# A decoder trunk on one core: second key group in two portions, attention's stores later, one split moved to VectorE

## The chip, the cores and the metric

The kernel runs on one core of one Trainium2 chip. A core has five engines, each with its own queue of instructions: TensorE (PE in the profile; PEld is its weight load), VectorE (DVE), ScalarE (ACT), GpSimd (POOL) and SyncE (SP), which here issues nearly all DMAs. The metric is the device time of one execution in microseconds (us); a kernel's time is the median of its runs.

## The reference, cut to what matters

The reference is one layer of a hybrid decoder over 2048 tokens of width 1024. All is fp32.

```python
u = x * (1.0 + scale[:, None, :]) + shift[:, None, :]
h = u @ w_in[l]
q, k, v, a_gate, p_in, p_gate, m_a, m_p = jnp.split(h, offsets, axis=-1)
a = sliding_window_sink_attention(q, k, v, sinks[l], bias, mask) * jax.nn.silu(a_gate)
a = a @ w_attn_proj[l]
p = jnp.einsum('bsgc,gcd->bsgd', multiscale_causal_pool(p_in), w_pool_mix[l]).reshape(B, S, POOL_WIDTH)
p = (p * pool_scale[l]) * jax.nn.silu(p_gate)
p = p @ w_pool_proj[l]
y = jax.nn.sigmoid(m_a) * a + jax.nn.sigmoid(m_p) * p
y = (y @ w_out[l]) * (1.0 + gate[:, None, :])
x = layer_norm(DEEPNORM_ALPHA * x + y, ln_gain[l], ln_bias[l])
```

Attention has 16 query heads of width 64 and 2 groups of keys and values, each shared by 8 query heads. A block of 128 queries sees its own block of 128 keys and the one before, with a bias by distance and a sink term in the softmax.

## The kernel before, in words

Every large matrix product is done by a seven-product scheme for 2 x 2 blocks (Winograd's form of Strassen's), and each fp32 operand is cut into a high and a low part, so that a product of two blocks is three TensorE passes (hi x hi, hi x lo, lo x hi, in `mm3`). The activations for one contraction stand in seven "sets" (`B11`, `T1`, `T2`, `B21`, `T3`, `B22`, `T4`), each with high and low parts. The weights of two output columns of 128 form a `Quad`. A quad passes through four stages: F (products with B11 and T1), S (T2, B21), Th (T3, B22) and L (T4). Each product is 12 matmuls of 128 x 512.

Before a stage's products, `split_part` cuts that stage's raw weights (tile `W`, or `A` for the last stage) into a high part by ScalarE and a low part `w_set<-W,w_set` by another engine: VectorE, but GpSimd for stage Th of quads that run alone. The sums that a stage needs (`W<-W`, `W<-W,A`) are GpSimd's. `plan` fixes, ahead of time, at which product each split, load and sum is given out. Every engine keeps to the order in which the program gives instructions out.

The sequence of 2048 tokens is done as two chunks of 1024 (s = 0 and 1). For each chunk there is a start phase, a middle phase `o` in which 13 quads run alone while attention is laid between their matmuls (`overlay`), and an end phase with quads in pairs; phases for the output projections and the norm follow. In `overlay` a `beat` comes after every three matmuls of a product, and some of the beats run one `step(n)` of attention. There are 64 steps for pairs of heads and blocks of 128 queries (plus three to run out): scores of n, transposes of n-2, values of n-3. The tile names are `lg` for scores, `L` for softmax rows, `pt` for transposes, `pv` for values, `st` for finished outputs, `kk` and `vv` for keys and values, `qs` for queries and `bt` for the bias.

The keys of one group lie in one buffer `kk` (one copy). Steps 0 to 31 use group 0 and steps 32 to 63 group 1. After step 31 `load_k(1)` gives out the loads of group 1 into the same buffer, and eight beats pass before step 32 is given out; the loads themselves wait until the scores of step 31 have read the old keys. After step 34 the same is done for `vv`. A tile's 64 + 64 partitions hold high and low parts for scores in two passes; in chunk 1 a tail of 128 columns of chunk 0's keys stands ahead of the chunk's 1024.

When four blocks of a pair of heads are done, `finish` multiplies by the gate (GpSimd, `st<-st,ag`), makes the sums that the later projection's sets need (`st<-st`), and gives out the stores `ain_d<-st` with `defer(ticks, ...)`: a tick is one product. SyncE takes its queue in order, so a store whose data are not ready holds back what stands behind it.

Of the kernel before, what the change touches and what calls it, by code (L numbers as in the profile page):

```python
# [19 lines left out]
P = 128  # L20
D = 1024
# [6 lines left out]
HD = 64  # L28
# [31 lines left out]
def kernel(  # L60
# [89 lines left out]
    def low(engine, dst, src, hi):  # L150
        engine.tensor_tensor(dst, src, as32(hi), ALU.subtract)
# [186 lines left out]
    def plan(phases):  # L338

        products, before, stages, order = [], {}, [], []  # L340
        for phase in phases:
            phase["base"], last = None, None
            for gi, grp in enumerate(phase["groups"]):
                if gi == 0:
                    phase["first"] = len(products)
                for x, q in enumerate(grp):
                    q.x, q.pair, q.own = x, len(grp) > 1, len(grp) > 1 and gi % 2 == 1
                    order.append(q)
                for kind, names in STAGES:
                    if kind == "S" and gi == 0:  # L350
                        phase["base"] = len(products)
                    if kind == "S" and gi == len(phase["groups"]) - 1:
                        phase["turn"] = len(products)
                    for q in grp:
                        if kind == "L" and not q.pair:
                            last = q
                            continue
                        p = len(products)
                        q.at[kind] = p
                        for h, name in enumerate(names):  # L360
                            products.append((q, kind, h, name))
                            if last and kind == "F" and h == 0:
                                last.at["L"] = len(products)
                                products.append((last, "L", 0, "T4"))
                        stages.append((q, kind, p, len(products) - 1))
                        if last and kind == "F":
                            stages.append((last, "L", last.at["L"], last.at["L"]))
                            last = None
            if last:
                last.at["L"] = len(products)  # L370
                stages.append((last, "L", len(products), len(products)))
                products.append((last, "L", 0, "T4"))
            phase["end"] = len(products)
# [43 lines left out]
    def split_part(ph, q, kind, part):  # L417
        raw = {"F": q.first, "S": q.second, "Th": q.third, "L": lambda: q.a22}[kind]()
        if kind == "L":
            if part == 0:  # L420
                t = q.parts["L"] = ph.split(*q.rings[kind])
                act.copy(t[:, 0:CH], raw)
            else:
                t = q.parts["L"]
                low(dve, t[:, CH:], raw, t[:, 0:CH])
            return
        if part == 0:
            hi, lo = q.parts[kind] = [ph.split(x) for x in q.rings[kind]]
            act.copy(by_two(hi), raw)
            return  # L430
        hi, lo = q.parts[kind]
        low(pool if kind == "Th" and not q.pair else dve, by_two(lo), raw, by_two(hi))
        if kind == "F":
            q.mid(pool)
            defer(2, lambda q=q: q.keep_sum(1))
        if kind == "S":
            q.late(pool)
# [299 lines left out]
    def overlay(ph, s, n_slots):  # L737
# [7 lines left out]
        def load_k(kv):  # L745
            k = kvt["k"] = tp.tile([P, 2, D + s * P], F32R, tag="kk", bufs=1, name="kk")
            mine = slice(kv * HD, (kv + 1) * HD)
            for half in range(2):
                at = slice(half * HD, (half + 1) * HD)
                if s:  # L750
                    sp.dma_start(as32(k[at, :, 0:P]), k_d[0, mine, :, D - P :])
                sp.dma_start(as32(k[at, :, s * P :]), k_d[s, mine])

        def load_v(kv):
            v = kvt["v"] = tp.tile([P, 2 * NB + s, P], F32R, tag="vv", bufs=1, name="vv")
# [63 lines left out]
        def finish(j, t):  # L819
            x, gate = outs[j, t], ags.pop((j, t))  # L820
            i, half = j // 2, j % 2
            pool.tensor_tensor(x, x, gate, ALU.mult)
            if (half, t) == (0, 1):
                b11 = outs[j, 0]
                pool.tensor_tensor(x, x, b11, ALU.subtract)
            if (half, t) != (1, 1):
                name = {(0, 0): "B11", (0, 1): "T1", (1, 0): "B21"}[half, t]
                defer(1, lambda: ain_d[s].put(name, i, x), True)
                return
            b11, t1, b21 = (outs.pop(z) for z in ((j - 1, 0), (j - 1, 1), (j, 0)))  # L830
            outs.pop((j, 1))
            pool.tensor_tensor(t1, x, t1, ALU.subtract)
            pool.tensor_tensor(b11, t1, b11, ALU.subtract)
            pool.tensor_tensor(b21, b21, t1, ALU.subtract)
            for name, z in (("B22", x), ("T2", t1), ("T3", b11), ("T4", b21)):
                defer(1, lambda name=name, z=z: ain_d[s].put(name, i, z), True)

        def step(n):
            lg = scores(n) if n < N else None
# [672 lines left out]
```

## Time and profile before

| | us |
|---|---|
| median of 3 runs | 1764.14 (1763.76 to 1764.63) |
| profiled execution, its own time | 1761.28 |
| its span, first to last instruction | 1759.5 |
| TensorE busy in it | 1673.6 |
| VectorE busy | 1276.9 |
| ScalarE busy | 939.8 |
| GpSimd busy | 591.2 |

Times inside the profile count from the first instruction. Attention of chunk 0 runs from about 176 to 517 us, of chunk 1 from about 776 to 1106 us. Nearly all operations pass through one helper, so they all carry line L56 and are told apart by their tiles. The mean granted TensorE clock of the profiled execution was 0.985 of full speed.

### The profile page before, as it was taken

The page shows a single profiled execution, that of the slowest core. Times are in us where ns is not written, and L with a number is a line of the kernel's source. Part 1 is how long each engine was busy: PE and PEld are TensorE (multiplying, and loading weights), DVE is VectorE, ACT ScalarE, POOL GpSimd, SP SyncE. Part 2 cuts the span into 40 slices and gives each one's busy share as a digit, 9 for nine tenths or more (in the row PEclk, how much of TensorE's full clock was granted, in tenths as well). Part 3 has the DMA queues.
Part 4 walks back from the last instruction along what each step waited for, and adds up shares of the span by engine and source line. Part 5 has one row for each costly group of instructions (what it writes and reads, how often), then busy time and mean ns, then how long its engine had stood idle before and what let it go on. Part 6 is the DMA issues. An engine that isn't in the chain of part 4 may idle for free.

```text
span 1759.5 us, 24784 instructions
## 1 busy us (share of the span) xinstructions
PE 1673.6 (95%) x8061; PEld 1399.2 (80%) x8061; DVE 1276.9 (73%) x2325; ACT 939.8 (53%) x1796; POOL 591.2 (34%) x564
## 2 busy tenths in 40 slices
PE   6899899999989999999999999999999999999996
PEld 5687688788878888888887888788888888888774
DVE  5854687677865879658786888387876785877677
ACT  3643587667763345447766676334544353435441
POOL 3022344454553322423333343322243211124442
PEclk9899899999999999999999999999999999999998
DMA  9288768666646889783555544489968686785332
GB/s 347 96 278 284 186 200 253 212 209 205 214 152 203 274 260 334 251 274 131 167 177 178 174 145 155 152 275 321 340 236 299 218 311 218 245 285 199 144 144 108
DMA packets 237010, 389.50 MB, mean 221 GB/s; under 512 B 21824, under 2 KB 90704, under 8 KB 236624
## 3 DMA queue, kind: packets, MB, share of 16 engines
q1 hardware_dynamic: 235664, 386.29, 65.9%
q10 hardware_dynamic: 1184, 1.60, 0.3%
q8 instruction: 63, 1.03, 0.2%
q14 instruction: 67, 0.55, 0.1%
q0 software_dynamic: 32, 0.02, 0.0%
HBM read 243.63 MB, written 147.35 MB: 222 GB/s over the span
## 4 chain that ended last, share of the span: by engine, by line
PE 63%; DVE 13%; DMA 7%; issue 6%; ACT 6%; POOL 2%; SPq 1%; POOLq 0%; DVEq 0%; ACTq 0%
PE mm L56 39%; PE lg L56 11%; PE c L56 8%; DVE w_set L56 3%; PE pt L56 3%; PE pv L56 3%; DVE L L56 2%; DVE wide L56 2%; ACT L L56 2%; ACT w_set L56 1%; SPq L56 1%; DMA q_d<-q_hi 1%; DMA wide<-in_xr_dram 1%; DVE set_T L56 1%; DVE p L56 1%
## 5 line engine op out<-in xcount | busy, mean ns | idle before, releaser
L56 PE MATMUL mm<-set_B,w_set 128*128 128x512 f32 x2664 | 654.9, 392 | 0.7 <-DVE w_set L56 0.6
L56 PEld LDWEIGHTS mm<-set_B,w_set 128*128 128x128 f32 x2664 | 498.7, 189 | 104.0 <-DVE w_set L56 1.0
L56 POOL TENSOR_TENSOR W<-W 128x512 f32<-128x512 f32 x185 | 267.7, 1457 | 590.7 <-DVE w_set L56 380.6
L56 PE MATMUL mm<-set_T,w_set 128*128 128x512 f32 x1824 | 454.8, 396 | 5.1 <-POOL w_set L56 4.4
L56 PEld LDWEIGHTS mm<-set_T,w_set 128*128 128x128 f32 x1824 | 341.8, 191 | 76.9 <-POOL w_set L56 5.3
L56 DVE TENSOR_TENSOR w_set<-W,w_set 128x1024 fp32r<-128x1024 f32 x196 | 253.5, 1293 | 113.9 <-ACT w_set L56 105.9
L56 ACT CAST w_set<-W 128x1024 fp32r<-128x1024 f32 x222 | 232.2, 1047 | 79.5 <-PE mm L56 52.6
L56 ACT ACTIVATE L<-L 128x257 f32<-128x257 f32 (+3 forms) x384 | 191.2, 500 | 120.1 <-DVE L L56 119.4
L56 PE MATMUL lg<-set_T,w_set 128*128 128x512 f32 x864 | 212.0, 393 | 6.4 <-ACT w_set L56 4.0
L56 PE MATMUL c<-set_T,w_set 128*128 128x512 f32 x864 | 211.1, 393 | 5.0 <-ACT w_set L56 2.9
L56 PEld LDWEIGHTS lg<-set_T,w_set 128*128 128x128 f32 x864 | 162.8, 190 | 43.4 <-ACT w_set L56 4.8
L56 PEld LDWEIGHTS c<-set_T,w_set 128*128 128x128 f32 x864 | 162.1, 189 | 41.6 <-ACT w_set L56 4.5
L56 POOL TENSOR_TENSOR W<-W,A 128x512 f32<-128x512 f32 x41 | 55.5, 1353 | 281.4 <-DMA A<-in_win_dram 115.5
L56 DVE CUSTOM_DVE_ANT_0 L<-lg,bt,nsink 128x256 f32<-128x256 f32 (+1 forms) x256 | 111.0, 469 | 26.6 <-PE lg L56 19.8
L56 PEld LDWEIGHTS lg<-kk,qs 128*128 128x128 f32 x512 | 76.7, 190 | 49.1 <-DVE L L56 26.1
L56 PE MATMUL lg<-kk,qs 128*128 128x256 f32 (+1 forms) x512 | 84.2, 287 | 30.0 <-DVE L L56 17.1
L56 DVE TENSOR_TENSOR ptl<-pt,pth 128x512 fp32r<-128x512 f32 (+1 forms) x128 | 85.8, 670 | 30.9 <-ACT pth L56 30.2
L56 DVE TENSOR_SCALAR L<-L 128x256 f32<-128x256 f32 (+1 forms) x128 | 98.2, 767 | 4.5
L56 ACT ACTIVATE sig<-mm 128x512 f32<-128x512 f32 x76 | 45.5, 599 | 92.7 <-PE mm L56 88.1
L56 ACT CAST pth<-pt 128x512 fp32r<-128x512 f32 (+1 forms) x128 | 72.3, 565 | 27.9 <-PE pv L56 27.1
L56 POOL TENSOR_TENSOR w_set<-W,w_set 128x1024 fp32r<-128x1024 f32 x26 | 63.3, 2435 | 56.5 <-ACT w_set L56 36.8
L56 PE MATMUL pt<-ident,L 128*128 128x128 f32 x496 | 77.9, 279 | 0.0
(203 smaller groups left out, 1943.9 us busy)
## 6 DMA issues: line engine op xcount, KB each, us to landing
W<-in_win_dram SPq DMA_DIRECT2D x40, 512.0 KB, 5.9
qs<-q_d SPq DMA_DIRECT2D x128, 128.0 KB, 4.3
sums_d<-W SPq DMA_DIRECT2D x62, 256.0 KB, 4.3
W<-sums_d SPq DMA_DIRECT2D x31, 512.0 KB, 3.7
ain_d<-st SPq DMA_DIRECT2D x56, 256.0 KB, 2.5
A<-in_win_dram SPq DMA_DIRECT2D x42, 256.0 KB, 5.4
ag_d<-sig SPq DMA_DIRECT2D x32, 256.0 KB, 4.6
q_d<-q_hi SPq DMA_DIRECT2D x32, 256.0 KB, 3.9
```

The lines of the kernel that those rows point to most:

```text
L56: return lambda *args, **kw: self.tc.keep_in_program_order(op(*args, **kw))
```

## The change

It has three parts.

1. `load_k`: for group 1 the keys are loaded in two portions. The first has columns 0 to 255 of the chunk (two blocks) for both halves of the partitions, the second the other 768. For group 0 nothing is cut. In chunk 1 the two tails of 128 columns now stand ahead of the rest.
2. `finish`: the stores of the sets B11, T1 and B21 come 2 ticks after `finish` rather than 1. Of the last four, B22 stays at 1, T3 and T2 come at 2 and T4 at 3, with T3 ahead of T2.
3. `plan` marks the quads of a phase's last group as `tail`; `split_part` gives the low part of stage Th of such a quad to VectorE, where it ran alone and so was GpSimd's. That is one quad in each chunk's attention phase. Quads in pairs had VectorE already.

```diff
+                    q.tail = gi == len(phase["groups"]) - 1
...
-        low(pool if kind == "Th" and not q.pair else dve, by_two(lo), raw, by_two(hi))
+        low(pool if kind == "Th" and not q.pair and not q.tail else dve, by_two(lo), raw, by_two(hi))
...
-            for half in range(2):
-                at = slice(half * HD, (half + 1) * HD)
-                if s:
+            ats = [slice(half * HD, (half + 1) * HD) for half in range(2)]
+            if s:
+                for at in ats:
                     sp.dma_start(as32(k[at, :, 0:P]), k_d[0, mine, :, D - P :])
-                sp.dma_start(as32(k[at, :, s * P :]), k_d[s, mine])
+            cut = 2 * P if kv else 0
+            for a, b in ((0, cut), (cut, D)):
+                for at in ats if a < b else ():
+                    sp.dma_start(as32(k[at, :, s * P + a : s * P + b]), k_d[s, mine, :, a:b])
...
-                defer(1, lambda: ain_d[s].put(name, i, x), True)
+                defer(2, lambda: ain_d[s].put(name, i, x), True)
...
-            for name, z in (("B22", x), ("T2", t1), ("T3", b11), ("T4", b21)):
-                defer(1, lambda name=name, z=z: ain_d[s].put(name, i, z), True)
+            for name, z, ticks in (("B22", x, 1), ("T3", b11, 2), ("T2", t1, 2), ("T4", b21, 3)):
+                defer(ticks, lambda name=name, z=z: ain_d[s].put(name, i, z), True)
```

SyncE's queue at the change of keys in chunk 0 (`kk` keys, `sums_d` kept weight sums, `ag_d` the attention gate; - is before, + now):

```order
 L56 DMA bt<-e_rep 128x2x256
-L56 DMA kk<-k_d 64x2048 x2
-L56 DMA sums_d<-W 128x512
-L56 DMA ain_d<-st 128x512
-L56 DMA ag_d<-sig 128x512 x2
+L56 DMA kk<-k_d 64x2x256 x2
+L56 DMA kk<-k_d 64x2x768 x2
+L56 DMA sums_d<-W 128x512
+L56 DMA ag_d<-sig 128x512
+L56 DMA ain_d<-st 128x512
+L56 DMA ag_d<-sig 128x512
 L56 DMA sums_d<-W 128x512
```

Two DMAs have become four, and a store of attention stands one place later.

VectorE at the end of chunk 0's attention, where the last quad's splits stand (`o` is the part of `pv` that ScalarE copied, `p` a partial sum). Before:

```order
L56 TENSOR_TENSOR w_set<-W,w_set 128x1024
L56 TENSOR_TENSOR ptl<-pt,pth 128x512
L56 TENSOR_TENSOR st<-pv,o_5278 64x128 x2
L56 TENSOR_TENSOR st<-pv,o_5306 64x128 x2
L56 TENSOR_TENSOR mm<-mm,p_5319 128x512
L56 TENSOR_TENSOR w_set<-A_4854,w_set 128x512
L56 TENSOR_TENSOR w_set<-W,w_set 128x1024
```

And now:

```order
L56 TENSOR_TENSOR w_set<-W,w_set 128x1024
L56 TENSOR_TENSOR ptl<-pt,pth 128x512
L56 TENSOR_TENSOR st<-pv,o_5280 64x128 x2
L56 TENSOR_TENSOR st<-pv,o_5308 64x128 x2
L56 TENSOR_TENSOR w_set<-W,w_set 128x1024
L56 TENSOR_TENSOR mm<-mm,p_5321 128x512
L56 TENSOR_TENSOR w_set<-A_4856,w_set 128x512
L56 TENSOR_TENSOR w_set<-W,w_set 128x1024
```

The added split stands between attention's last outputs and the accumulation `mm<-mm,p`; GpSimd's queue has lost the same instruction behind its three `st<-st`.

SyncE's queue at the same place, before:

```order
L56 DMA ma_d<-sig 128x512
L56 DMA ain_d<-st 128x512 x4
L56 DMA W<-in_win_dram 128x512
L56 DMA W<-in_win_dram 128x2x512
L56 DMA u_d<-ux 128x4x256
L56 DMA A_5374<-in_win_dram 128x512
```

And now:

```order
L56 DMA ma_d<-sig 128x512
L56 DMA ain_d<-st 128x512
L56 DMA W<-in_win_dram 128x512
L56 DMA W<-in_win_dram 128x2x512
L56 DMA u_d<-ux 128x4x256
L56 DMA ain_d<-st 128x512 x2
L56 DMA A_5375<-in_win_dram 128x512
L56 DMA ain_d<-st 128x512
```

Three of the four stores now stand behind the loads of the next quad's weights.

## The prediction

> **What bounds the kernel now.** I read the page's busy times first, then the list of TensorE's waits, then the order of time at each long wait.
>
> ```profile
> PE 1673.6 (95%) x8061; PEld 1399.2 (80%) x8061; DVE 1276.9 (73%) x2325; ACT 939.8 (53%) x1796; POOL 591.2 (34%) x564
> ...
> PE lg L56 <- DVE L L56: 17.1, 18, 3.0
> PE mm L56 <- POOL w_set L56: 4.4, 2, 2.8
> PE lg L56 <- DMA ain_d<-st: 3.5, 1, 3.5
> PE lg L56 <- DMA kk<-k_d: 2.5, 1, 2.5
> ```
>
> TensorE (PE) is busy for 95% of the span, so a microsecond counts only where TensorE itself stands still. The waits are in us in total, times, longest. The change can reach three of these rows: 2.5, 3.5 and 4.4 us. The largest, scores behind VectorE's softmax (17.1 us in 18 pieces), it doesn't touch directly.
>
> The order of time around the change of keys, TensorE's rows, chunk 0 and then chunk 1 (start, length, and in brackets the idle time before):
>
> ```profile
> 343.08 0.96 PE L56 MATMUL lg<-kk,qs 128*128 128x128 f32 x4 [2.50 <-DMA kk<-k_d]
> 349.49 0.64 PE L56 MATMUL lg<-kk,qs 128*128 128x256 f32 x4
> 354.32 0.62 PE L56 MATMUL lg<-kk,qs 128*128 128x256 f32 x4
> ...
> 936.62 0.82 PE L56 MATMUL lg<-kk,qs 128*128 128x256 f32 x4 [3.51 <-DMA ain_d<-st]
> 943.14 0.64 PE L56 MATMUL lg<-kk,qs 128*128 128x256 f32 x4
> 947.98 0.62 PE L56 MATMUL lg<-kk,qs 128*128 128x256 f32 x4
> ...
> 936.61 0.53 PEld L56 LDWEIGHTS lg<-kk,qs 128*128 128x128 f32 x4 [3.93 <-DMA kk<-k_d]
> ```
>
> In both chunks TensorE does the products that the beat lets through, then stands still until the second group's keys are there: from 340.58 (343.08 - 2.50), and from 933.11. The second wait is put down to a store that landed at nearly the same moment; the weight load's own row names the keys, and that is what I take.
>
> A stall has a second price. Granted clock (PEclk) in stretches around the two:
>
> ```profile
> 340.00:343.00 3.00, 0.58 (x3) 1.00 0.91 290
> 343.00:346.00 3.00, 2.92 (x14) 0.54 0.99 356
> 937.00:940.00 3.00, 3.00 (x14) 0.52 0.80 257
> 522.00:526.00 4.00, 1.25 (x6) 1.00 0.35 131
> ```
>
> Columns: stretch, its length, PE busy with its instructions, PEclk, share of the DMA engines, GB/s. Behind each key wait the clock is near half. So one attention step, from scores to scores, takes 343.08 to 349.49 = 6.41 us and 936.62 to 943.14 = 6.52 us, where the next steps take 4.83 (to 354.32) and 4.84 us (to 947.98). That is 1.58 and 1.68 us on top of the stalls.
>
> **Part 1, keys in two portions.** What SyncE issues there, and how long the keys took to land:
>
> ```profile
> 334.33 0.37 SPq L56 DMA_DIRECT2D bt<-e_rep  x1
> 334.80 1.11 SPq L56 DMA_DIRECT2D kk<-k_d  x2
> ...
> 927.24 2.46 SPq L56 DMA_DIRECT2D kk<-k_d  x4
> ...
> DMA to landing us min/median/max: 5.5/6.5/7.6
> ...
> DMA to landing us min/median/max: 2.7/5.5/7.5
> ...
> DMA to landing us min/median/max: 2.9/2.9/2.9
> ```
>
> The landing rows are the keys of chunk 0, those of chunk 1, and the bias bt just ahead (the same 2.9 in both chunks). In chunk 0 bt lands at 334.33 + 2.9 = 337.2, the first 512 KB at 334.8 + 5.5 = 340.3 and the second at 342.9: some 2.8 us per 512 KB. The first portion is two pieces of 128 KB, 0.7 us each by that rate: landed by about 338.7. TensorE comes at 340.58, so 1.9 us are left. In chunk 1 the tails (64 KB each, 128 columns) go first, then two pieces of 128 KB: 384 KB behind bt at 929.7. The old 1,152 KB took from there to 936.6, 6.9 us; a third is 2.3 us, so they land at 932.0, and TensorE comes at 933.11: 1.1 us left. I take no wait in either. The bounds come from the landing rows: with 2.7 us from the last first-portion issue (335.3 and 929.1) it is 338.0 and 931.8; with the 7.6 and 7.5 us that the last halves needed it is 342.9 and 936.6, and nothing is gained.
>
> What is late next: the second portion is 768 KB, 4.2 us at the old rate, so it lands at about 343 and 937. It is first read two steps on, at 340.58 + 2 x 4.83 = 350.2 and 933.11 + 2 x 4.84 = 942.8. The queries of that same step are closer.
>
> ```profile
> 342.82 1.25 SPq L56 DMA_DIRECT2D qs<-q_d  x2
> 932.38 2.11 SPq L56 DMA_DIRECT2D qs<-q_d  x2
> ...
> DMA to landing us min/median/max: 4.4/4.4/4.5
> ...
> DMA to landing us min/median/max: 6.1/6.7/7.2
> ```
>
> Issued at 342.8 (second one 343.5) and landing in 4.5, they are there at 348.0, and at 932.4 + 7.2 or 933.9 + 6.1 = 940.0 in chunk 1. The two added DMAs stand ahead of them in SyncE's queue, 2 x 0.6 us (2.46 / 4 each); if that delays them in full, it is 349.2 and 941.2: still 1.0 and 1.6 us early. Part 1 then gains 2.50 + 1.58 = **4.08** and 3.51 + 1.68 = **5.19**. The reordering at the start of chunk 1's attention (tails first) has the same bytes ahead of the same scores: 0.
>
> **Part 2, the split of the last quad.** The end of chunk 0's attention, by engine:
>
> ```profile
> 514.88 1.05 ACT L56 CAST w_set<-W 128x1024 fp32r<-128x1024 f32 x1 [0.63 <-POOL W L56]
> 516.36 0.58 DVE L56 TENSOR_TENSOR st<-pv,o 64x128 f32<-64x128 f32 x2 [1.80 <-ACT o L56]
> 518.83 4.35 POOL L56 TENSOR_TENSOR st<-st 128x512 f32<-128x512 f32 x3
> 519.70 0.70 DVE L56 TENSOR_TENSOR mm<-mm,p 128x512 f32<-128x512 f32 x1 [2.76 <-PE mm L56]
> 520.43 1.60 DVE L56 TENSOR_TENSOR w_set<-A,w_set 128x512 fp32r<-128x512 f32 x1
> 523.14 2.34 POOL L56 TENSOR_TENSOR w_set<-W,w_set 128x1024 fp32r<-128x1024 f32 x1
> 525.53 2.58 PE L56 MATMUL mm<-set_T,w_set 128*128 128x512 f32 x10 [2.75 <-POOL w_set L56]
> ...
> 1113.74 2.57 PE L56 MATMUL mm<-set_T,w_set 128*128 128x512 f32 x10 [1.63 <-POOL w_set L56]
> ...
> L56 DVE TENSOR_TENSOR w_set<-W,w_set 128x1024 fp32r<-128x1024 f32 x196 | 253.5, 1293 | 113.9 <-ACT w_set L56 105.9
> ```
>
> The high part is ready at 515.93, but GpSimd's low part stands behind its operations on the finished heads (to 523.18) and ends at 525.48; T3's third matmul waits 2.75 us for it. In chunk 1 it is 1.63 us. VectorE is idle from 516.94 to 519.70, just where the new instruction stands. Its 1.29 us ends at 518.2 when alone. Beside GpSimd these operations stretch (the 128x512 one took 1.60 us), to 2.64 us at most in this stage by VectorE's next split (523.91, below): 519.6, still 3.2 us ahead of 522.78, where TensorE stopped. The accumulation mm<-mm,p behind it slips by nothing or some tenths; B22, which reads it, comes a product (2.7 us) after T3. Later VectorE work is the next quad's split:
>
> ```profile
> 523.91 2.64 DVE L56 TENSOR_TENSOR w_set<-W,w_set 128x1024 fp32r<-128x1024 f32 x1 [1.88 <-ACT w_set L56]
> ```
>
> It ends at 526.55 at the latest, and T3, B22 and T4, three products, keep TensorE until about 522.15 + 3 x 2.72 = 530.3. So 2.75 + 1.63 = **4.38** is gained; if the cover were gone and VectorE paid in full, 2 x 1.29 would go back. GpSimd is free 2.3 us sooner, and the W buffer with it, which SyncE's next loads waited for: off the path.
>
> **Part 3, stores later.** The bytes are the same and no TensorE wait names these stores, apart from the one explained above. SyncE stood behind GpSimd's heads for 55.6 us:
>
> ```profile
> SPq L56 <- POOL st L56: 55.6, 39, 3.3
> ```
>
> That blocking goes, so the loads behind it are issued up to 3.3 us sooner. They were not late, so 0; but it can shift when GpSimd adds weights beside VectorE. What that is worth, either way, is shown by the worst such meeting:
>
> ```profile
> 395.14 1.38 DVE L56 TENSOR_SCALAR L<-L 128x128 f32<-128x128 f32 x1
> 395.18 1.26 POOL L56 TENSOR_TENSOR W<-W 128x512 f32<-128x512 f32 x1 [8.59 <-DVE L L56]
> 397.39 0.88 PE L56 MATMUL lg<-kk,qs 128*128 128x256 f32 x4 [3.05 <-DVE L L56]
> ```
>
> 3.05 us and some 1.6 for the clock behind it, 4.6 either way. I take 0 and keep 4.6 for both ends.
>
> **The sum.** 4.08 + 5.19 + 4.38 = 13.65 us. The profiled execution took 1761.28 us (span 1759.5 and 1.8 around it): 1747.6. It lay 2.86 us below the median of the runs shown, 1764.14; with the same distance the median becomes **1750.5 us**.
>
> **Rivals.** *Keys still late* (10%): the DMA share is 0.91 and more just there, and everything issued around 335 landed 7 us later; or the scores wait for the whole tile. Late in chunk 1 alone, where the margin is 1.1: 1764.14 - 4.08 - 4.38 = 1755.7; in both, 1759.8. Against it: bt, just ahead, needed 2.9.
>
> *VectorE gives back the split* (8%): the low part meets GpSimd's operations one after another and T3, or what VectorE does next, is late by what was won: 1764.14 - 9.27 = 1754.9. Against it stand the 3.2 us of room. [...]
>
> *The slow clock isn't the stall's doing* (5%): TensorE also paused 2.75 us before 525.53 and the clock stayed at 1.00. If the half-clock stretches stay, 1.58 + 1.68 are not gained: 1753.8. The rows at 343 and 937, each right behind a stall, speak against it. [...]
>
> *Slower* (4%): loads that come earlier move GpSimd's weight sums onto VectorE's row scaling, as at 395. Each costs 4.6; it takes four of them in the two attentions to outweigh 13.65 by more than 0.2%: 1750.5 + 18.4 = 1768.9. With three it is a draw. Only two stalls of this size stand in the trace, and GpSimd's start hangs mostly on VectorE (the 8.59 above), not on loads.
>
> *The time is taken back* (3%): a later stage fed by DMA ends when it did: 1764. Against it: that stage's loads are released by this same stream, and TensorE's row above has 95%.
>
> **How the numbers follow.** The forecast has the other 70%; its own range is 1746 to 1755, which holds a 4.6 either way. To hold 8 in 10 I add the late keys of one chunk and the split given back: **1746 to 1757.5**. A measurement of this kernel can tell about 0.2%, 3.5 us, from no change. Faster than 1760.6: 70 + 8 + 5 and most of 10, **91%**; within 0.2%, the rest and the time taken back, **5%**; slower **4%**.
>
> **What would show it.** Right: scores with the new keys follow the products with no wait above 0.5 us in both chunks, and PEclk there stays near 1.00; first-portion landings of about 3 us; no TensorE wait for w_set at either end of attention; VectorE's added split over before T2's product ends. Wrong: a wait for kk or qs one or two steps later; a TensorE idle time in front of T3 now put down to VectorE; or the list's "PE lg <- DVE L" well above 17.1 us, which would take the gain back in small pieces.

## The result, and the profile after

Measured side by side, four runs each, the kernel took 1764.39 us before (1763.76 to 1764.69) and 1749.1 us with the change (1746.87 to 1751.48). The ratio is 0.9923, 95% interval 0.9907 to 0.9938: 13.6 us, between 10.9 and 16.4 (the two medians lie 15.3 us apart). The prediction said 1750.5 us, range 1746 to 1757.5, and a gain of 13.65. The profiled execution of the changed kernel took 1751.48 us, the longest of its four, and the one before 1761.28, so the two profiles lie only 9.8 us apart. Measured again, beside its own runs of the kernel before, the changed kernel had 0.9934 (0.992 to 0.9949).

Busy time on the page of the changed kernel (engine, us, share of the span, instructions):

```profile
span 1749.7 us, 24770 instructions
...
PE 1672.3 (96%) x8061; PEld 1398.1 (80%) x8061; DVE 1278.1 (73%) x2327; ACT 939.7 (54%) x1796; POOL 590.5 (34%) x562
```

TensorE does the same 8061 matmuls in nearly the same busy time, 1672.3 us against 1673.6. What went is time in which it stood still: span less busy was 85.9 us before and is 77.4 now, 8.5 of the 9.8 us between the two spans.

TensorE's waits by what was waited for (us in total, times, longest), now:

```profile
PE lg L56 <- DVE L L56: 18.1, 18, 2.9
```

Only the largest of the four rows shown of before has its like here; 17.1 us became 18.1, still in 18 pieces. The row for the keys and the row `PE mm L56 <- POOL w_set L56` are gone. The order of time shows it at the change of keys, first chunk 0, then chunk 1 (TensorE's rows; the idle time would stand in brackets):

```profile
341.99 0.56 PE L56 MATMUL lg<-kk,qs 128*128 128x128 f32 x4
...
346.75 0.64 PE L56 MATMUL lg<-kk,qs 128*128 128x256 f32 x4
...
351.58 0.62 PE L56 MATMUL lg<-kk,qs 128*128 128x256 f32 x4
...
360.37 0.36 PE L56 MATMUL pv<-pth,vv 128*128 128x256 f32 x1 [0.35 <-DMA vv<-v_d]
...
926.32 0.64 PE L56 MATMUL lg<-kk,qs 128*128 128x256 f32 x4
...
931.14 0.63 PE L56 MATMUL lg<-kk,qs 128*128 128x256 f32 x4
...
935.98 0.64 PE L56 MATMUL lg<-kk,qs 128*128 128x256 f32 x4
```

The first scores with the new keys (341.99 and 926.32) have no wait in front of them, and the step that took 6.41 and 6.52 us now takes 346.75 - 341.99 = 4.76 and 931.14 - 926.32 = 4.82. One new wait stands there, 0.35 us, and it names a tile that the prediction never priced: the values `vv`, needed for the first time by the step's `pv` product. The granted clock in the stretches (stretch, length, busy time and count of PE, PEld, DVE, ACT, POOL, then the clock, the share of the DMA engines, GB/s):

```profile
340.00:343.00 3.00, 3.00 (x20) 2.65 (x19) 2.08 (x7) 1.46 (x3) 2.73 (x3) 1.00 1.00 256
343.00:346.00 3.00, 3.00 (x17) 2.56 (x16) 1.38 (x5) 2.61 (x9) 3.00 (x5) 1.00 1.05 396
929.00:932.00 3.00, 3.00 (x20) 2.60 (x18) 1.78 (x7) 2.58 (x7) 1.02 (x1) 1.00 1.08 363
```

PE is busy for all of each stretch and the clock is 1.00, where it was 0.54 and 0.52. What SyncE issues there now, and the time from issue to landing of the first portion (chunk 0's two DMAs, then the two tails and the two pieces of the first portion in chunk 1):

```profile
336.38 2.47 SPq L56 DMA_DIRECT2D kk<-k_d  x4
...
920.62 3.76 SPq L56 DMA_DIRECT2D kk<-k_d  x6
...
DMA to landing us min/median/max: 3.1/3.4/3.7
...
DMA to landing us min/median/max: 2.5/2.8/2.9
```

The last piece that the first scores need was issued at 337.0 and 922.5 and landed by 337.0 + 3.7 = 340.7 and 922.5 + 2.9 = 925.4. TensorE came at 341.99 and 926.32: 1.3 and 0.9 us of room.

The end of chunk 0's attention, by engine:

```profile
512.31 0.58 DVE L56 TENSOR_TENSOR st<-pv,o 64x128 f32<-64x128 f32 x2 [1.80 <-ACT o L56]
...
512.93 1.60 DVE L56 TENSOR_TENSOR w_set<-W,w_set 128x1024 fp32r<-128x1024 f32 x1
...
513.41 2.27 POOL L56 TENSOR_TENSOR st<-st,ag 128x512 f32<-128x512 f32 x1
...
515.76 4.23 POOL L56 TENSOR_TENSOR st<-st 128x512 f32<-128x512 f32 x3
...
518.09 2.92 PE L56 MATMUL mm<-set_T,w_set 128*128 128x512 f32 x12
...
519.86 1.22 DVE L56 TENSOR_TENSOR w_set<-W,w_set 128x1024 fp32r<-128x1024 f32 x1 [2.27 <-ACT w_set L56]
```

VectorE's added split takes 1.60 us and is over at 514.53, 3.6 us before T3 (518.09), which now runs its twelve matmuls in one piece. GpSimd is still at the finished heads until 519.99; before, the split stood behind that.

**Where the time went.** Start of the same TensorE instruction in the two profiled executions, in order of the program:

| at | before | after | after less before |
|---|---|---|---|
| scores early in chunk 0's attention | 197.21 | 198.90 | +1.7 |
| first scores with new keys, chunk 0 | 343.08 | 341.99 | -1.1 |
| a few products later | 346.42 | 343.79 | -2.6 |
| first product with new values | 362.52 | 360.37 | -2.2 |
| half-clock stretch at 398 not met | 401.38 | 397.26 | -4.1 |
| T3 at the end of chunk 0's attention | 525.53 | 518.55 | -7.0 |
| first scores with new keys, chunk 1 | 936.62 | 926.32 | -10.3 |
| a few products later | 940.61 | 928.63 | -12.0 |
| T3 at the end of chunk 1's attention | 1113.74 | 1101.61 | -12.1 |
| last phase | 1724.30 | 1713.99 | -10.3 |

From just ahead of each place to just behind it, the change's own steps are -4.3 around the keys of chunk 0 (+1.6 to -2.7), +0.6 at the values, -3.0 at the first T3 (-4.1 to -7.1), -5.3 around the keys of chunk 1 (-6.6 to -12.0) and -1.9 at the second T3 (-10.3 to -12.2): 13.9 us. The rest is half-clock stretches that fall elsewhere in one execution than in the other (3.4 us each, at 1066, 1626 and 1711 now; at 398 and 1681 before). The +1.7 at the head, ahead of every edit, comes from them too: at 102 us the two executions were level within 0.2 us, and the one now went on at half clock until 106.8 and was 1.85 us behind by then. Between single executions these are worth a few us (about half of each stretch's 3.4 us, as an estimate from a clock of 0.50 from 398 to 401 before); the medians average over them.

### The profile page after: what moved, and what is told of

It is laid out like the page before. It is cut to its first block, busy times and chain, and to the rows that moved or that the text cites. A ratio compares the mean times of both kernels' runs of the same rounds, so it can differ in the third digit from the quotient of the medians.

```text
span 1749.7 us, 24770 instructions
## 1 busy us (share of the span) xinstructions
PE 1672.3 (96%) x8061; PEld 1398.1 (80%) x8061; DVE 1278.1 (73%) x2327; ACT 939.7 (54%) x1796; POOL 590.5 (34%) x562
## 4 chain that ended last, share of the span: by engine, by line
PE 63%; DVE 11%; DMA 7%; ACT 6%; issue 5%; POOL 1%; SPq 1%; POOLq 0%; DVEq 0%; ACTq 0%
PE mm L56 38%; PE lg L56 11%; PE c L56 9%; DVE w_set L56 3%; PE pv L56 3%; PE pt L56 2%; DVE L L56 2%; DVE wide L56 2%; ACT L L56 2%; ACT w_set L56 1%; SPq L56 1%; DMA qs<-q_d 1%; DMA wide<-in_xr_dram 1%; DVE p L56 1%; ACT sig L56 1%
## 5 line engine op out<-in xcount | busy, mean ns | idle before, releaser
L56 PE MATMUL mm<-set_B,w_set 128*128 128x512 f32 x2664 | 657.6, 394 | 1.1 <-DVE w_set L56 0.8
L56 PEld LDWEIGHTS mm<-set_B,w_set 128*128 128x128 f32 x2664 | 500.6, 190 | 105.6 <-DVE w_set L56 1.7
L56 POOL TENSOR_TENSOR W<-W 128x512 f32<-128x512 f32 x185 | 267.2, 1454 | 593.0 <-DVE w_set L56 411.6
L56 PE MATMUL mm<-set_T,w_set 128*128 128x512 f32 x1824 | 451.8, 394 | 0.7 <-DVE set_T L56 0.7
L56 PEld LDWEIGHTS mm<-set_T,w_set 128*128 128x128 f32 x1824 | 340.1, 190 | 71.1 <-DVE set_T L56 2.3
L56 DVE TENSOR_TENSOR w_set<-W,w_set 128x1024 fp32r<-128x1024 f32 x198 | 255.9, 1292 | 115.7 <-ACT w_set L56 112.5
L56 ACT CAST w_set<-W 128x1024 fp32r<-128x1024 f32 x222 | 232.1, 1047 | 82.2 <-PE mm L56 52.0
L56 ACT ACTIVATE L<-L 128x257 f32<-128x257 f32 (+3 forms) x384 | 191.2, 500 | 118.7 <-DVE L L56 118.0
L56 PE MATMUL lg<-set_T,w_set 128*128 128x512 f32 x864 | 213.3, 395 | 6.3 <-ACT w_set L56 3.6
L56 PE MATMUL c<-set_T,w_set 128*128 128x512 f32 x864 | 212.9, 395 | 5.1 <-ACT w_set L56 3.0
L56 PEld LDWEIGHTS lg<-set_T,w_set 128*128 128x128 f32 x864 | 163.2, 190 | 43.8 <-ACT w_set L56 4.8
L56 PEld LDWEIGHTS c<-set_T,w_set 128*128 128x128 f32 x864 | 163.3, 190 | 42.1 <-ACT w_set L56 4.6
L56 POOL TENSOR_TENSOR W<-W,A 128x512 f32<-128x512 f32 x41 | 58.0, 1415 | 278.1 <-DMA A<-in_win_dram 128.9
L56 DVE CUSTOM_DVE_ANT_0 L<-lg,bt,nsink 128x256 f32<-128x256 f32 (+1 forms) x256 | 111.0, 469 | 20.7 <-PE lg L56 14.5
L56 PEld LDWEIGHTS lg<-kk,qs 128*128 128x128 f32 x512 | 76.6, 189 | 43.0 <-DVE L L56 26.6
L56 PE MATMUL lg<-kk,qs 128*128 128x256 f32 (+1 forms) x512 | 83.5, 285 | 24.7 <-DVE L L56 18.1
L56 DVE TENSOR_TENSOR ptl<-pt,pth 128x512 fp32r<-128x512 f32 (+1 forms) x128 | 85.7, 670 | 28.8 <-ACT pth L56 27.8
L56 DVE TENSOR_SCALAR L<-L 128x256 f32<-128x256 f32 (+1 forms) x128 | 98.4, 769 | 4.5
L56 ACT ACTIVATE sig<-mm 128x512 f32<-128x512 f32 x76 | 45.5, 599 | 91.4 <-PE mm L56 86.8
L56 ACT CAST pth<-pt 128x512 fp32r<-128x512 f32 (+1 forms) x128 | 72.3, 565 | 20.1 <-PE pv L56 19.1
L56 POOL TENSOR_TENSOR w_set<-W,w_set 128x1024 fp32r<-128x1024 f32 x24 | 58.2, 2424 | 56.6 <-ACT w_set L56 35.3
L56 PE MATMUL pt<-ident,L 128*128 128x128 f32 x496 | 76.9, 277 | 0.0
```

The lines of the kernel that those rows point to most:

```text
L56: return lambda *args, **kw: self.tc.keep_in_program_order(op(*args, **kw))
```

## The experiments

Each batch with its own runs of the kernel before on the same chip: 1761.02 us in the first, 1760.34 in the second, 1761.41 in the third.

| batch | kernel | median us | of before | 95% interval |
|---|---|---|---|---|
| 1 | keys in two portions alone | 1753.02 | 0.9955 | 0.994 to 0.9969 |
| 1 | split on VectorE alone | 1754.19 | 0.9963 | 0.9947 to 0.998 |
| 1 | stores later alone | 1759.6 | 0.9994 | 0.998 to 1.0008 |
| 1 | keys and split, stores as before | 1749.31 | 0.9937 | 0.9917 to 0.9958 |
| 2 | the changed kernel again | 1748.33 | 0.9934 | 0.992 to 0.9949 |
| 2 | changed, large portion first | 1751.66 | 0.9957 | 0.9941 to 0.9973 |
| 2 | changed, first portion 512 columns | 1751.77 | one run | |
| 2 | changed, row scaling later | 1723.89 | 0.9799 | 0.9781 to 0.9816 |
| 3 | the same again | 1725.59 | 0.9791 | 0.9773 to 0.9809 |
| 3 | changed, values in two portions | 1747.26 | 0.9912 | 0.9892 to 0.9931 |
| 3 | changed, row scaling later and values in two | 1722.14 | 0.9779 | 0.9761 to 0.9797 |
| 3 | before, row scaling later alone | 1733.58 | 0.9841 | 0.9824 to 0.9859 |

**Each part alone.** The theory is the sum of the prediction: three waits of TensorE that have nothing to do with one another, so their prices add. First the keys:

```diff
+            cut = 2 * P if kv else 0
+            for a, b in ((0, cut), (cut, D)):
+                for at in ats if a < b else ():
+                    sp.dma_start(as32(k[at, :, s * P + a : s * P + b]), k_d[s, mine, :, a:b])
```

> The kernel before with the keys in two portions alone. Theory (the gain is the sum of TensorE's own stalls, each with the slow clock behind it): both waits for kk go, 2.50 + 1.58 and 3.51 + 1.68, so 9.3 us less than before, about 1755.1 us; the waits for w_set at the ends of attention stay at about 2.7 and 1.6 us. Rival (the parts need each other: the stores that now leave later are what lets the first portion through in time): some wait for kk stays, and the gain is under 6 us.

Then the split:

```diff
-        low(pool if kind == "Th" and not q.pair else dve, by_two(lo), raw, by_two(hi))
+        low(pool if kind == "Th" and not q.pair and not q.tail else dve, by_two(lo), raw, by_two(hi))
```

> The kernel before with the last quad's low part on VectorE alone. Theory: the two waits for w_set (2.75 and 1.63) go and nothing takes their place: 4.4 us less, about 1760.0 us; the key waits stay at 2.5 and 3.5. Rival (what counts at the end of attention is that the next quad's loads no longer stand behind four stores): T3 waits less, but TensorE waits a product or two later for weights, and the gain is under 2 us.

Then the stores:

```diff
-                defer(1, lambda: ain_d[s].put(name, i, x), True)
+                defer(2, lambda: ain_d[s].put(name, i, x), True)
...
-            for name, z in (("B22", x), ("T2", t1), ("T3", b11), ("T4", b21)):
-                defer(1, lambda name=name, z=z: ain_d[s].put(name, i, z), True)
+            for name, z, ticks in (("B22", x, 1), ("T3", b11, 2), ("T2", t1, 2), ("T4", b21, 3)):
+                defer(ticks, lambda name=name, z=z: ain_d[s].put(name, i, z), True)
```

> The kernel before with the later stores alone. Theory: nothing, within 1 us of before, with TensorE's waits for kk (2.5, 3.5) and w_set (2.75, 1.63) all still there. Rival (the stores are worth the 1.6 us by which the median gained more than the 13.65 forecast, or more): 1.6 to 4 us less than before.

And the first two together, which is the changed kernel with its stores put back:

> The changed kernel with the stores as before. Theory: keys and split add up, 13.7 us less than before, about 1750.7 us, as the changed kernel within 1.5 us. Rival (the stores carry part of it): 1.6 to 4 us slower than the changed kernel, so 1751 to 1753.5 us against its 1749.1, and with waits for kk or w_set left.

Against 1761.02 us the keys alone gave 7.9 us (5.5 to 10.6), the split alone 6.5 (3.5 to 9.3), the stores alone 1.1 (1.4 the other way to 3.5). The first two add to 14.4, the pair measured 11.1 (7.4 to 14.6). So they add as far as these intervals tell, and the stores are worth nothing that can be measured: the pair has 0.9937, the whole change 0.9923 and 0.9934.

The traces say which wait each part takes. TensorE in order of time, keys alone:

```profile
359.63 0.36 PE L56 MATMUL pv<-pth,vv 128*128 128x256 f32 x1 [1.00 <-DMA vv<-v_d]
...
520.90 3.58 PE L56 MATMUL mm<-set_T,w_set 128*128 128x512 f32 x10 [2.79 <-POOL w_set L56]
...
1105.27 2.57 PE L56 MATMUL mm<-set_T,w_set 128*128 128x512 f32 x10 [1.64 <-POOL w_set L56]
```

No key is waited for, both waits for GpSimd's split are there. With the split alone it is the other way round:

```profile
340.89 0.63 PE L56 MATMUL lg<-kk,qs 128*128 128x128 f32 x4 [2.15 <-DMA sums_d<-W]
...
930.64 1.22 PE L56 MATMUL lg<-kk,qs 128*128 128x256 f32 x4 [2.81 <-DMA ain_d<-st]
```

Both of these stand at the first scores with the new keys, as in the kernel before; they are put down to stores that landed at nearly the same moment.

Part 3 took away a wait of SyncE's, and in part only moved it. SyncE's time behind GpSimd's finished heads was 55.6 us in 39 pieces, and behind GpSimd's writes to the softmax rows (`POOL L`) 60.2 in 27. In the changed kernel:

```profile
SPq L56 <- POOL L L56: 74.2, 26, 7.7
...
SPq L56 <- POOL st L56: 23.5, 18, 3.3
```

The one row lost 32 us and the other gained 14; all of SyncE's waits together went from 1122 to 1109 us. The time did not change by anything that can be measured.

**Which portion first.** If TensorE waited because the whole tile had to land, cutting it helps only when the part that is read first comes first:

```diff
-            for a, b in ((0, cut), (cut, D)):
+            for a, b in ((cut, D), (0, cut)):
```

> The changed kernel with the two portions of group 1 in the other order, the 768 columns first. Same bytes, same four DMAs. Theory (what counts is that the columns read first also land first): the first portion lands last, at about 343 and 937 in the time of before, so the waits of about 2.5 and 3.5 us are back, and it is 6 us slower than the changed kernel, up to 9.3 when the slow clock follows both. Rival (smaller pieces, or four DMAs in flight, land sooner whatever their order): no wait over 1 us, time as the changed kernel.

TensorE's waits with the large portion first:

```profile
PE lg L56 <- DMA kk<-k_d: 4.9, 2, 3.3
```

Both waits for keys are back, 1.59 us in chunk 0 and 3.30 in chunk 1, and the kernel has 0.9957 where the changed one beside it has 0.9934. The difference, 0.0023 of 1760 or 4.0 us, is smaller than the 6 expected and the 9.27 that the prediction gave the keys, and the intervals overlap, so the time alone would not settle it; the waits do. The DMAs are the same in number and shape, so it is the order that takes the waits away.

**How large the first portion.**

```diff
-            cut = 2 * P if kv else 0
+            cut = 4 * P if kv else 0
```

> The changed kernel with a first portion of 512 columns in place of 256, 256 KB a piece. Theory (landing goes by the bytes ahead, some 0.7 us for 128 KB): in chunk 0 it lands at 337.2 + 2.8 = 340.0, no wait or up to 0.3 us; in chunk 1 640 KB behind the bias at 163 KB/us land 3.9 us later, at 933.6, so the scores wait about 0.5 us. Rival (a fixed delay of some 3 us whatever the size): no wait in either.

One run: 1751.77 us. In chunk 0 there is no wait: the last piece of the first portion landed 5.2 us after the first issue, as the theory has it, where the eight traces with 256 columns have 3.8 to 4.4. In chunk 1 TensorE stood still for 0.40 us:

```profile
929.26 0.71 PE L56 MATMUL lg<-kk,qs 128*128 128x256 f32 x4 [0.40 <-issue]
```

The profile names no releaser here, but the last piece landed at 929.06, 0.2 us ahead of the scores, so I read it as a wait for keys. It does not show what the size costs, though. That piece landed 6.1 us after the first issue; with keys and split alone, at 256 columns, it was 6.1 us as well, with a wait of 0.41, and in the other seven traces 4.6 to 5.3. So in chunk 1 the theory stays open, and the room is thin there with 256 columns too.

**The values.** The new wait for `vv` was 0.35 us in the first profile of the changed kernel. The changed kernel again, with nothing edited:

> The changed kernel once more, on the chip of the runs beside it. Theory (keys and split add, stores add nothing): as e4_keys_split, 0.993 of before within 0.002.

TensorE at the same product in this execution:

```profile
355.89 0.36 PE L56 MATMUL pv<-pth,vv 128*128 128x256 f32 x1 [2.25 <-ACT L L56]
```

and the granted clock behind it:

```profile
357.00:360.00 3.00, 3.00 (x9) 2.33 (x8) 1.94 (x7) 2.96 (x8) 1.87 (x3) 0.54 0.93 272
```

Here it is 2.25 us, with a clock of 0.54 behind. The name in brackets is ScalarE's, but the values, issued at 347.56, landed 8.2 us later, at 355.76, just ahead of the product. In the kernel before they landed at 359.9 and the product came at 362.5, so 2.6 us were left. In the changed kernel's first profile they were issued 2.0 us sooner than before (353.69 against 355.67) and yet landed 0.3 us later (360.23), while TensorE came 2.5 us sooner. So part of what the keys gain in chunk 0, 0.35 to 2.25 us and in that execution a stretch of slow clock, is lost again one transfer later. Are they late because the whole tile is waited for?

```diff
-            sp.dma_start(as32(v[:, s:]), v_d[s, :, kv])
+            cut = 2 if kv else 0
+            for a, b in ((0, cut), (cut, 2 * NB)):
+                if a < b:
+                    sp.dma_start(as32(v[:, s + a : s + b]), v_d[s, :, kv, a:b])
```

> The changed kernel, with the second group's values (vv) loaded in two portions too, blocks 0 and 1 first. Theory (once the keys are in time, the values are what is late next, and only because the whole tile is waited for): the wait of pv for vv in chunk 0, 0.35 us in the changed kernel's first profile and 2.25 in its second, is gone, and the time is 0 to 3 us below the changed kernel's 1748 to 1749, 0.990 to 0.9935 of the kernel before. Rival (the values are late because the queries and keys ahead of them in SyncE's queue are, whatever their size): the wait stays within half a us of what it was and the time does not move.

TensorE at the same product, values in two portions:

```profile
360.68 0.36 PE L56 MATMUL pv<-pth,vv 128*128 128x256 f32 x1 [0.16 <-DMA vv<-v_d]
```

The first portion, a quarter of the tile, landed 0.2 us behind the queries that were issued just before it (360.54 and 360.37) and the second 0.9 later. So cutting is worth at most that 0.9 us. The rest of the 6.9 us from issue to landing goes, as far as this trace tells, to the queue of transfers ahead, with the DMA engines nearly always at work (from 350 to 356 us packets took 97.8% of their time). The time, 0.9912, cannot be told from 0.9934 and 0.9923: the intervals overlap.

**The clock behind a stall.** The prediction put 1.58 and 1.68 us of slow clock on top of the two key waits, and its third rival held that the stall has nothing to do with it. Both are answered by two kernels that still have the wait for keys in chunk 0: stores later alone, and the kernel before with the row scaling later (below). TensorE in the first:

```profile
341.99 0.64 PE L56 MATMUL lg<-kk,qs 128*128 128x128 f32 x4 [2.54 <-DMA kk<-k_d]
```

its stretches around the wait:

```profile
339.00:342.00 3.00, 0.47 (x3) 0.07 (x2) 0.01 (x1) 1.35 (x2) 3.00 (x4) 1.00 0.94 306
342.00:345.00 3.00, 3.00 (x19) 2.71 (x20) 1.52 (x7) 1.50 (x5) 2.04 (x3) 1.00 0.97 359
```

TensorE in the second:

```profile
335.91 0.64 PE L56 MATMUL lg<-kk,qs 128*128 128x128 f32 x4 [1.93 <-DMA sums_d<-W]
```

and its stretches:

```profile
334.00:337.00 3.00, 1.09 (x10) 1.12 (x11) 0.41 (x3) 1.03 (x2) 2.82 (x4) 1.00 1.01 365
337.00:340.00 3.00, 3.00 (x11) 2.51 (x10) 1.65 (x6) 2.41 (x8) 2.66 (x2) 0.51 1.02 327
```

The longer stall, 2.54 us, is followed by full clock, the shorter one, 1.93 us, by half. Length alone does not decide. How a stall lies against the recorded clock differs as well. In the trace of the kernel before, half-clock stretches of 3.413 us begin at 343.22, 397.83, 486.58 and 937.14, a whole number of 3.413 us apart (16, 26 and 132 of them). Laid out from there in pieces of that length, that trace has the stall of 2.50 us (340.58 to 343.08) whole within one piece (339.80 to 343.22, idle for 73%), and half clock follows; the stall of 2.75 us in front of T3 (522.78 to 525.53) is cut by a border at 524.12, one piece idle for 39% and the next for 41%, and full clock follows. The stall of 1.93 us (333.98 to 335.91) lies as the first of these does: by the 0.51 in the stretch from 337 to 340 half clock begins there at about 337.05, and the stall fills 57% of the 3.413 us ahead of it.

From 160 us on, the last half-clock stretch of each trace left out, this trace and the first one of the changed kernel, in pieces laid out the same way, have 14 (not themselves at half clock) in which TensorE stood still for 44% or more. All 7 with 62% or more were followed by a piece at half clock, and 4 of the 7 with 44 to 52%; of those with 41% or less, none. The count rests on two executions and on modelled ends of matmuls. It is an observation; no kernel was made to move a stall against the pieces.

So, as far as these runs show, the price of a stall of this size is a matter of chance. The wait for GpSimd's split in chunk 0 shows it too: no slow clock in the kernel before (2.75 us), but with the keys alone the ten matmuls behind its 2.79 us took 3.58 us instead of 2.58, at a clock of 0.52 from 522 to 525. The prediction charged the clock to the keys and nothing to the split, as the one execution had it. Over many runs the keys should then get a little less and the split a little more, which is the direction of 7.9 against 9.27 and of 6.5 against 4.38. But both forecasts lie within the measured intervals, so this is argued and not shown.

**The wait that the change does not touch.** The largest row, scores behind VectorE's softmax, was kept by the prediction as a risk of 4.6 us. At its worst place VectorE scales the rows of the step before (`TENSOR_SCALAR L<-L`) in front of its reads of the new scores, and TensorE waits for the bank that these reads free. The changed kernel again, TensorE, VectorE and GpSimd in order of time:

```profile
389.84 1.38 DVE L56 TENSOR_SCALAR L<-L 128x128 f32<-128x128 f32 x1
389.88 1.26 POOL L56 TENSOR_TENSOR W<-W 128x512 f32<-128x512 f32 x1 [8.64 <-DVE L L56]
...
391.14 0.47 DVE L56 CUSTOM_DVE_ANT_0 L<-lg,bt,nsink 128x256 f32<-128x256 f32 x1
...
391.55 0.48 DVE L56 CUSTOM_DVE_ANT_0 L<-lg,bt,nsink 128x256 f32<-128x256 f32 x1
...
392.08 1.23 PE L56 MATMUL lg<-kk,qs 128*128 128x256 f32 x4 [3.10 <-DVE L L56]
```

The scaling starts with GpSimd's sum and ends with it, after 1.38 us; a larger one (128x256) takes 0.35 where GpSimd does nothing beside it (397.66 in the last fence of this part). In the whole first profile of the changed kernel 54 of the 128 scalings had no GpSimd operation beside them, and none of these took more than 0.36 us; ahead of each of its 18 waits stood one that took 1.0 to 1.5 us beside GpSimd. What makes a scaling long beside GpSimd's sum no run here shows. The edit gives the scaling out behind the reads:

```diff
-                dve.tensor_scalar(E[:, 1, e0:256], E[:, 1, e0:256], sm[:, 1:2], None, ALU.mult)
+                scaled = E[:, 1, e00:256], smm[:, 1:2]
...
                 Es[n] = L, e0, sm
+            if scaled:
+                dve.tensor_scalar(scaled[0], scaled[0], scaled[1], None, ALU.mult)
```

> The changed kernel with VectorE's row scaling of the step before given out after the reads of the new scores, not ahead of them. It touches the waits the change left: scores behind VectorE's softmax, 16 us in 15 places. Theory (there VectorE's row scaling stands 1.2 to 1.4 us behind GpSimd's weight sum, ahead of the read that frees the scores' buffer): these waits fall to under 7 us, and the time is 6 to 11 us less than the changed kernel. Rival (VectorE as a whole is late there, and the order inside a step doesn't matter): waits and time within 2 us of the changed kernel.

The gain was larger than the 6 to 11 us expected, and the list on the page of the changed kernel had 18.1 us in 18 places to lose, not 16 in 15: 1723.89 us, 24.4 below the changed kernel beside it, and 1725.59 once more in another batch. TensorE's busy row and its row for this wait, first the changed kernel again:

```profile
PE 1669.2 (96%) x8061; PEld 1395.8 (80%) x8061; DVE 1279.6 (73%) x2327; ACT 939.4 (54%) x1796; POOL 590.0 (34%) x562
...
PE lg L56 <- DVE L L56: 17.7, 18, 3.1
```

then with the scaling later:

```profile
PE 1661.3 (97%) x8061; PEld 1395.9 (81%) x8061; DVE 1251.1 (73%) x2327; ACT 935.6 (54%) x1796; POOL 589.2 (34%) x562
...
PE lg L56 <- DVE L L56: 0.3, 1, 0.3
```

The whole list went, 17.7 - 0.3 = 17.4 us, and not only its worst pieces; and TensorE's own busy time fell by 7.9 us, the same matmuls at a mean granted clock of 0.988 instead of 0.984. The two make 25.3, and the spans differ by 1746.6 - 1721.5 = 25.1. Over the two attentions (176 to 520 and 776 to 1106 us) the mean clock is 0.99 and 1.00 with the scaling later, and 0.98 and 0.99 in the changed kernel again. Later, the scaling may be as slow as it likes:

```profile
391.43 0.64 PE L56 MATMUL lg<-kk,qs 128*128 128x256 f32 x4
...
392.52 0.49 DVE L56 CUSTOM_DVE_ANT_0 L<-lg,bt,nsink 128x256 f32<-128x256 f32 x1
...
392.92 2.14 DVE L56 TENSOR_SCALAR L<-L 128x256 f32<-128x256 f32 x1
...
396.02 0.64 PE L56 MATMUL lg<-kk,qs 128*128 128x256 f32 x4
...
397.66 0.35 DVE L56 TENSOR_SCALAR L<-L 128x256 f32<-128x256 f32 x1
```

One of 2.14 us, longer than the one that cost 3.10, and the next scores follow without a wait. Most of the stretching stayed, too: the 128 scalings took 98 us in all in the changed kernel again and 82 us here. So the place in VectorE's queue alone was worth more than the whole change. The kernel once more, for the comparisons that follow:

> The changed kernel with VectorE's row scaling behind its reads of the new scores, once more, beside the other three: 1722 to 1726 us, 0.978 to 0.982 of the kernel before.

**Does the change still pay without that wait?** The kernel before with the same edit, and nothing of the change:

> The kernel before with the row scaling later alone; nothing of the change. Theory (the change's three waits have nothing to do with VectorE's row scaling, so the parts add): the kernel with both is 1723.9 and the change was worth 12 to 15 us, so 1735 to 1739 us, 0.986 to 0.989 of the kernel before; the waits for kk stand in both chunks, longer than before by up to 2 us because TensorE reaches them sooner, which would make the change worth up to 4 us more here. Rival (TensorE's time lost by the row scaling and by the keys is partly one time): the kernel is within 5 us of 1724.

TensorE's waits there:

```profile
PE mm L56 <- POOL w_set L56: 3.7, 2, 2.1
...
PE lg L56 <- DMA kk<-k_d: 2.0, 1, 2.0
PE lg L56 <- DMA sums_d<-W: 1.9, 1, 1.9
```

1733.58 us, 1.4 us below the expected band. The three waits of the change are there (the second and third rows are the keys in chunk 1 and chunk 0), but shorter, 7.6 us in all against 10.4 in the kernel before, and not longer as expected. On this kernel the change is worth 1733.58 - 1725.59 = 8.0 us. By the two ratios it is 8.8 us, and by their intervals some 4 to 13. On the kernel before it was 11.6 (0.9934) and 13.6 (0.9923). So the parts add as far as these runs tell, and the theory's second half, that the keys would be waited for longer, fell: both rows are shorter than 2.50 and 3.51 us. Why the keys come earlier relative to TensorE here was not followed up.

**Both edits together.** Row scaling later, values in two portions:

> Row scaling later and the values in two portions. If the two add: 0 to 2 us below the kernel with the row scaling alone (1723.9), since the wait for vv measured 0.60 us there; if the values' second portion, or the DMA added in SyncE's queue, comes late for something else, 0.5 to 2 us above it.

1722.14 us against 1725.59 beside it, intervals 0.9761 to 0.9797 and 0.9773 to 0.9809, so not told apart; it is the lowest median of all. The wait for the values did not go, TensorE at that product:

```profile
352.50 0.36 PE L56 MATMUL pv<-pth,vv 128*128 128x256 f32 x1 [1.12 <-DMA vv<-v_d]
```

It was 0.60 and 0.93 us with the values in one piece. Again the first portion landed 0.2 us behind the queries ahead of it (352.37 and 352.18), which themselves needed 8.2 us. Here the rival is right: what is late is the queue, and the cut of the tile is worth no more than the 0.9 us by which the second portion landed later (353.23). Issuing the values earlier was not tried. There is little to win without more memory: the tile has one buffer (`bufs=1`), and in the profile of the changed kernel the last product with the old values ended at 352.90 and the new ones were issued at 353.69.

## Why the prediction was right, step by step

**The sum: right, and in part by luck.** 13.65 us foreseen and 13.6 measured, but the interval is 10.9 to 16.4, and the two terms measured alone lie off in opposite directions, though each forecast is within the measured interval: 7.9 us for the keys (9.27 foreseen) and 6.5 for the split (4.38). The mechanism behind each term held; that the sum came so close was luck.

**Keys in two portions: right in kind and nearly in size.** Both waits went, the first pieces landed 4.3 us after the first issue in chunk 0 (3.9 foreseen) and 4.8 in chunk 1 (4.8), and the room was 1.3 and 0.9 us (1.9 and 1.1). One of the eight traces with this cut still waited 0.41 us in chunk 1. In the profiled pair the steps are 4.3 and 5.3 us (4.08 and 5.19). Over many runs the part alone has 7.9 (5.5 to 10.6) where 9.27 was foreseen: the term of the slow clock is paid in some executions and not in others, and in chunk 0 something goes back to the values. Both point that way; how much each takes was not measured.

**"What is late next": wrong name.** The prediction looked at the second portion and at the queries. The second portion landed at 344.15, 7.4 us before 351.58; the queries of that step landed at 348.77, 2.8 us early (1.0 foreseen), in chunk 1 at 933.85, 2.1 us before 935.98 (1.6). The step that failed is that it stopped there. The values, given out three steps later in the same queue, had 2.6 us of room before (359.9 to 362.5), less than the 4.08 that the keys were to gain. The list of room was not carried that far; what it missed measured 0.35 to 2.25 us.

**The split: right.** 1.60 us between the bounds of 1.29 and 2.64; room 3.6 us (3.2); no wait for `w_set` at either end; in the profiled pair 3.0 and 1.9 us (2.75 and 1.63). Alone it measured 6.5 (3.5 to 9.3) where 4.38 was foreseen: a stall of 2.8 us costs slow clock in some executions (0.52 behind the 2.79 us with the keys alone, 1.00 behind the 2.79 us with the stores alone), which this step left out because the one execution had none. Whether that is the whole difference the interval does not tell.

**Stores later: right.** Nothing measurable either way, 0.9994 (0.998 to 1.0008). That the blocking goes was half right: 23.5 of 55.6 us stayed, and 14 us came back behind `POOL L`. The 4.6 us kept for both ends were not needed for this part; the row for VectorE's softmax went from 17.1 to 18.1 us.

**The rivals.** Late keys (apart from the 0.41 us above), a split given back and the time taken back are refuted by the traces and times above. "The slow clock isn't the stall's doing" is half right: in the traces of the kernel before and of the changed one each half-clock stretch from 160 us on begins behind 3.413 us in which TensorE stood still for 44% or more, but a stall of this size does not always bring one (half clock behind 1.93 and 2.50 us, full clock behind 2.54 and 2.75). The rival on the slower side had the right mechanism, scaling beside GpSimd's sum, and the wrong reading of it: it asked how the change would move such meetings, when they held 18 waits and some 25 us that a change of order could take away.

## What to carry to other kernels

Where a wait for a load is taken away, list the room of every load behind it in the same queue, and not of the next one alone; the first with less room than the gain is where the gain stops. Where an engine frees a bank that TensorE waits for, put the freeing reads ahead of everything that engine can do later: here that order was worth 24 us, twice the three parts together. A price of the slow clock read from one execution is one draw: charge every stall of that size (1.9 to 2.8 us here, where half clock followed 1.93, 2.50 and 2.79 us and full clock 2.54, 2.75 and 2.79) with a part of it, not those alone that paid it in the profile.

## What was not expected of the hardware

The half-clock stretches of the kernel before were 3.413 us long each, once three times that and at the very end longer; in the changed kernel three were twice 3.413 us, and they lay elsewhere. A stall of 1.93 us was followed by one, stalls of 2.54 and 2.75 us were not; of the pieces of 3.413 us idle for 62% and more all 7 were. The ten matmuls behind the same wait of 2.79 us took 3.58 us with the keys alone and 2.57 with the stores alone.

With the values in two portions, the time from issue to landing of the values followed what stood ahead of them: the first portion landed 0.2 us behind the queries issued just before, 6.9 and 7.2 us after its issue in the two kernels, and the other three quarters needed only 0.9 us more. In the first of the two the DMA engines were at work for 97.8% of the time from 350 to 356 us.
